# Layer 1's output projection: a fifth unit by seven products, and a new order of the products

## The chip, the core and the metric

The kernel runs on one core of one Trainium2 chip. Its time is device time in microseconds (us), from one execution of the whole program; three timed runs of the kernel before gave a median of 1409.27 us (1408.67 to 1409.78). Beside them stands one profiled execution, whose trace all durations below come from.

The engines are TensorE (PE; PEld is its loading of stationary operands), VectorE (DVE), ScalarE (ACT), GpSimd (POOL) and SyncE (SP). Each works through its own instructions in the order in which the program has them. POOL and SP here mostly issue DMA transfers.

## The reference, cut to what matters

A model of two layers on 512 tokens of width 1024, in float32. Each layer is a mixer (dilated attention in layer 0, an mLSTM in layer 1) and a SwiGLU block; a last RMS norm follows. What the change touches is the second matrix product of the SwiGLU block of layer 1, with the residual and the norm behind it:

```python
def swiglu(xn, w_in, w_out):
    gu = xn @ w_in
    return (jax.nn.silu(gu[..., :D_FF]) * gu[..., D_FF:]) @ w_out
...
        h = h + swiglu(rms_norm(h, ffn_norm[i]), ffn_w_in[i], ffn_w_out[i])
    return rms_norm(h, final_norm)
```

So the output projection is a product of a hidden matrix of 512 x 2816 with `w_out` of 2816 x 1024.

## The kernel before

**Precision.** Every matrix product is computed as three products of halves: each float32 operand is split into a high part (a rounding copy on ACT, L209 for weights, L1120 for activations) and a low part (a subtraction on DVE, L210 for weights, L1109 for activations), and high x high, high x low and low x high are added up in PSUM (`SPLITS`).

**The layer's first product.** `ffn_in` computes the hidden matrix `hid` in 11 pairs of 128-row chunks (`hid[0]` to `hid[10]`), the last eight of them by seven products instead of eight (L1017). While it runs, `during` (L1248) prepares sums of the hidden matrix for the second product, and the last of its steps already prepare that product's first operands.

**The output projection.** `output_products` (L1087) plans it for both layers. Take a quarter problem: rows k of `w_out` in two halves, tokens in two halves of 256, output columns in two halves of 512. Eight products of quarters would be needed; with sums and differences of the operands seven do (P1 to P7), whose results are added up in PSUM. A *unit* u is one such set of seven products; it couples the row pairs `hid[u]` and `hid[UNITS + u]`. With `UNITS = 4` in layer 1, four units cover 8 of the 11 row pairs, and the remaining three (`REST`) are computed plainly, for each of the two column halves: "first" (columns 512 and up) and "second" (columns below 512). Layer 0 has `sums_of_rows` true and `UNITS = 5`.

One product is 12 matmuls of 128 x 128 by 128 x 512 in layer 1 (`multiply_half`, L1697: two token tiles, two k-chunks, three splits); a plain rest item is 24 in the loop. The order is written out by hand (L1265 to L1269): P1 of all units, P5 and P2 in turn, P6 of all units, P7 with the "first" rest items between, P3, P4, and the three "second" rest items at the end.

**Where the sums of weights come from.** Each unit has one weight tile `T` (`f1T` in the trace), loaded by SP at P1 (L1174). P1, P5, P6 and P4 split it in place. Behind the split at P1 and at P5 it is negated on ACT (L1166) and another row block is added to it by a DMA with addition that POOL issues (L1163, 512 KB); at P6 it is only negated; at P7 a freshly loaded block is added to it on DVE (L1189: the block's tile becomes the sum) and POOL adds a further block to `T` for P4. P2, P3, P7 and the rest load their block by SP into one of three buffers `wraw` (L201). The split results, high and low, take one of three buffers each (`whi`, `wlo`), given out in the order of the items: the split of item i + 2 can begin when PE has finished item i - 1.

**What limits the order.** `prepare` (L1271) puts the preparation of an item two items ahead of its product (`AHEAD = 2`); a scheduler then fixes one order of instructions for each engine, by its own estimates.

**PSUM.** P1 and P2 add into `c11`, P5 and P3 into `p5`, P6, P7 and P4 into `u_`. At four points a finished sum is carried over: `copy_banks(u_, c11)` behind the last P1 and `copy_banks(c22, p5)` behind the last P5 (ACT), `add_banks((0, 1), u_)` behind the last P6 and `add_banks((2, 3), u_)` in `after_p7` behind the last P7 (DVE, L1726, `ht <- finu`). They are keyed by the last unit's number, 3. The next product that writes to `u_` must wait for the DVE addition that reads it. `outputs` (behind P4_0 and P4_1) adds the residual for columns 512 and up and squares it for the norm.

**The end.** The last three items (`TAIL = 3`, before: second_0 to second_2) are not run in the loop but tile by tile (from L1750 on): token tiles 0, 1, 2, then tile 3 in two halves of 256 columns, so that a tile's residual (L1709), square (L1711), root (L1771, Newton step L1772 to L1774), scaling (L1776 on ACT, L1778 on DVE, gains L1713 on POOL) and output DMA run beside the next tile's matmuls. A "product" among the last items concerns tiles 2 and 3 only:

```python
            todo = [e for e in last if tb >= 2 or e[0] == "rest"]
```

Of the kernel before, what the change touches and what calls it, by code (L numbers as in the profile page):

```python
# [12 lines left out]
F32R = mybir.dt.float32r  # L13
# [4 lines left out]
P = 128  # L18

SEQ = 512  # L20
# [51 lines left out]
def tile_hybrid_dilated_attn_mlstm(  # L72
# [5 lines left out]
    x = x[0]  # L78
# [6 lines left out]
    xp = pool(ctx, "act")  # L85
# [258 lines left out]
    h = [hp.tile([P, SEQ], F32, tag="h", name="h%d" % k, bufs=KC + 1) for k in range(KC)]  # L344
# [745 lines left out]
    def output_products(layer, fp, wo, sums_of_rows):  # L1090
# [3 lines left out]

        UNITS = 5 if sums_of_rows else 4
        TAIL = 3
        REST = range(2 * UNITS, FC // 2)
        hid, ops, whl, sums, tw, w8 = [], {}, {}, [], [], []  # L1100
# [4 lines left out]
        def half(pi, t):  # L1105
            return hid[pi][:, :, t * HALF:(t + 1) * HALF]

        def subtract(out, x, y):
            nc.vector.tensor_tensor(out, x, y, op=ALU.subtract)  # L1109

        def split_operand(name, u, src):

            i = UNITS * (PARTS.index(name) % 3) + u
            nm = "f%d%s_%d" % (layer, name, u)
            if i < 2 * len(PRODUCTS):
                t = fp.tile([P, 2, 2, HALF], F32R, tag="op%d" % i, name=nm)
                hi, lo = t[:, 0], t[:, 1]
            else:
                hi, lo = [fp.tile([P, 2, HALF], F32R, tag="gu0", name=nm, bufs=3) for _ in range(2)]
            nc.scalar.activation(hi, src, AF.Copy)  # L1120
            subtract(lo, src, hi.bitcast(F32))
            ops[name, u] = [[t[:, k] for k in range(2)] for t in (hi, lo)]
# [31 lines left out]
        def prepare_product(name, u):  # L1154
            nm = "f%d%s_%dw" % (layer, name, u)
            view = lambda t: t.rearrange("p (k n) -> p k n", k=2)

            def load(hk, n):
                return load_chunk(weight_rows(hk * UNITS + u, n), [P, 2, 512], nm)[0]

            def add_rows(to, hk, n):

                nc.gpsimd.dma_start(view(to), weight_rows(hk * UNITS + u, n), accum_op=ALU.add)  # L1163

            def negate(x):
                nc.scalar.activation(x, x, AF.Copy, scale=-1.0)  # L1166
            if name == "P1":
                if u < 4:
                    if u % 2 == 0:
                        w8.append(fp.tile([P, 2, 1024], F32, tag="w8", name="f%dT%d" % (layer, u), bufs=2))  # L1170
                    tw.append(w8[-1][:, u % 2])
                else:
                    tw.append(fp.tile([P, 1024], F32, tag="t1", name="f%dT%d" % (layer, u)))
                nc.sync.dma_start(view(tw[u]), weight_rows(u, 0))  # L1174
            t = tw[u]
            in_place = ("P1", "P6", "P3") if sums_of_rows else ("P1", "P5", "P6", "P4")
            if sums_of_rows and name == "P5":
                prepare_first_sum(u, t, nm)
                return
            raw = t if name in in_place else load(*ROWS[name])  # L1180
            if sums_of_rows:

                if name == "P7":
                    nc.vector.tensor_tensor(raw, raw, t, op=ALU.add)
                    add_rows(t, 1, 0)


            elif name == "P7":
                nc.vector.tensor_tensor(raw, raw, t, op=ALU.add)  # L1189
                add_rows(t, 1, 0)  # L1190
            whl[name, u] = split_chunk((raw, 1024, view, nm))
            if sums_of_rows and name == "P1":

                for i in {0: (0,), 1: (1,), UNITS - 1: range(2, UNITS)}.get(u, ()):
                    load_first_sum(i)
            if sums_of_rows:
                if name == "P6":
                    negate(t)
            elif name in ("P1", "P5"):
                negate(t)  # L1200
                add_rows(t, int(name == "P5"), 1)
            elif name == "P6":
                negate(t)

            if (name, u) in ops:
                return
            if name == "P1":
                split_operand(name, u, half(u, 0))
            elif name == "P2":
                split_operand(name, u, half(UNITS + u, 0))  # L1210
            elif name == "P5":
                split_operand(name, u, sums[u])
            elif name == "P6":
                split_operand(name, u, half(u, 1))

                subtract(sums[u], half(u, 1), half(u, 0) if sums_of_rows else half(UNITS + u, 1))
            elif name == "P7":
                split_operand(name, u, sums[u])
            elif name == "P3":
                if not sums_of_rows:  # L1220
                    subtract(half(u, 1), half(UNITS + u, 0), half(u, 1))
                split_operand(name, u, half(UNITS + u, 1) if sums_of_rows else half(u, 1))
            elif name == "P4":
                if sums_of_rows:
                    subtract(half(UNITS + u, 0), half(UNITS + u, 0), half(u, 1))
                split_operand(name, u, half(UNITS + u, 0 if sums_of_rows else 1))

        def prepare_rest(n, pi):
            if pi not in ops:
                i = pi - REST[0]  # L1230
                two = lambda name, *tags: [fp.tile([P, SEQ], F32R, tag=tg, name="f%dh%s%d" % (layer, name, pi), bufs=bufs)
                                           for tg, bufs in tags]
                if sums_of_rows:
                    hi, lo = two("h", ("gu1", 2), ("gu1", 2)), two("l", ("u2", 1), ("v5", 1))
                else:

                    p, tag = (fp, "op%d" % (3 * UNITS + i)) if i < 2 else (xp, "x%d" % (pi - 4))
                    t = p.tile([P, 2, SEQ], F32R, tag=tag, name="f%dhh%d" % (layer, pi))
                    hi = [t[:, k] for k in range(2)]
                    lo = two("l", *((("u2", 1), ("v5", 1)) if i == 0 else (("gu%d" % (2 - i), 1 + i),) * 2))  # L1240
                for k in range(2):
                    nc.scalar.activation(hi[k], hid[pi][:, k], AF.Copy)
                    subtract(lo[k], hid[pi][:, k], hi[k].bitcast(F32))
                ops[pi] = hi, lo
            whl[n, pi] = split_chunk(load_chunk(weight_rows(pi, n), [P, 2, 512], "f%dw%d_%d" % (layer, n, pi)))

        def during(j, i):
# [12 lines left out]
            if j == FC - 2 and i == 6:  # L1260
# [4 lines left out]
        order = ("P1_0 P1_1 P1_2 P1_3 P1_4 P5_0 P2_0 P5_1 P2_1 P6_0 P5_2 P2_2 P6_1 P5_3 P2_3 P6_2 P5_4 P2_4 P6_3 P6_4 "  # L1265
                 "P7_0 first_0 P7_1 P7_2 P3_0 P7_3 P3_1 P7_4 P3_2 P3_3 P4_0 P3_4 P4_1 P4_2 P4_3 P4_4 second_0"
                 if sums_of_rows else
                 "P1_0 P1_1 P1_2 P1_3 P5_0 P2_0 P5_1 P2_1 P5_2 P2_2 P5_3 P2_3 P6_0 P6_1 P6_2 P6_3 P7_0 first_0 P7_1 first_1 "
                 "P7_2 first_2 P7_3 P3_0 P3_1 P3_2 P3_3 P4_0 P4_1 P4_2 P4_3 second_0 second_1 second_2").split()  # L1269
        items = []  # L1270
        for e in order:  # L1271
            name, i = e.split("_")
# [27 lines left out]
    with ExitStack() as fctx:  # L1300
        fp = pool(fctx, "ffn0")
        hid, during, prepare, work = output_products(0, fp, ffn_w_out[0], True)
# [24 lines left out]
        old, h = h, []  # L1327
# [16 lines left out]
        def first_tiles():  # L1344
            for m in range(4):
                natural(m, F[0][m])
        last = work(product, plain, {("P1", 4): lambda: copy_half(0), ("P5", 4): lambda: copy_half(1),
                                     ("P6", 4): lambda: add_sum(0), ("P7", 4): lambda: add_sum(1),
                                     ("P4", 2): first_tiles})
# [8 lines left out]
    with ExitStack() as mctx:  # L1358
# [138 lines left out]
        i = 0  # L1497
# [154 lines left out]
    with ExitStack() as fctx:  # L1652
        fp = pool(fctx, "ffn1")
        dp = pool(fctx, "scratch1", space=bass.MemoryType.DRAM)
        R = 32
        hid, operands, prepare, work = output_products(1, fp, ffn_w_out[1], False)
# [17 lines left out]
        for n in (1, 0):  # L1674
            for tb in range(TB):
                t = ht[tb, n] = hp.tile([P, SEQ], F32, tag="h", name="ht%d_%d" % (tb, n), bufs=KC + 1)
# [18 lines left out]
        c11, u_ = [bank("s", "c11") for _ in range(2)], [bank("acc", "u") for _ in range(2)]  # L1695
# [24 lines left out]
        def copy_banks(to, src):  # L1720
            for m in range(2):
                nc.scalar.activation(to[m], src[m], AF.Copy)

        def add_banks(tbs, src):
            for m, tb in enumerate(tbs):
                nc.vector.tensor_tensor(ht[tb, 1], src[m], ht[tb, 1], op=ALU.add)  # L1726
# [12 lines left out]
        def plain(n, pi, a, w):  # L1739
            for t in range(2):  # L1740
                multiply_half(((c11, u_), (p5, c22))[n][t], a, t, w)

        last = work(product, plain, {("P1", 3): lambda: copy_banks(u_, c11), ("P5", 3): lambda: copy_banks(c22, p5),
                                     ("P6", 3): lambda: add_banks((0, 1), u_), ("P7", 3): after_p7,
                                     ("P4", 0): lambda: outputs((0, 1), p5), ("P4", 1): lambda: outputs((2, 3), c22)})

        rest_of = bank("o", "last")
        t = ht[TB - 1, 0][:, 256:]
# [55 lines left out]
```

## Time and profile before

| | us |
|---|---|
| median of the three timed runs | 1409.27 (1408.67 to 1409.78) |
| the profiled execution's own time | 1408.68 |
| its span, first to last instruction | 1406.9 |
| PE busy in the span | 1394.5 (99%) |
| DVE / ACT / POOL busy | 1054.9 (75%) / 665.4 (47%) / 149.0 (11%) |
| granted TensorE clock, mean | 0.999 |
| output projection of layer 1 on PE, first to last matmul | 1290.59 to 1399.94 |

How to read it: the profiled execution took 1.8 us more than its span, which lies around the span and isn't seen in it. A busy share is an average over all stages. Matmuls are pipelined, so that one of 128 x 512 shows a duration of 0.39 us while the next starts 0.23 us later; what a product costs is therefore read from starts, not from durations. Rows of a timeline give start, duration, engine, line, operation, output <- inputs, and in brackets how long the engine sat idle before and what released it.

### The profile page before, as it was taken

How to read it: one execution, taken by the hardware profiler on the slowest of the kernel's cores; microseconds unless marked ns; L12 is line 12 of the kernel's file. 1: busy time of each engine (PE TensorE's matmuls, PEld its weight loads, DVE VectorE, ACT ScalarE, POOL GpSimd, SP SyncE). 2: the span in 40 equal slices, each digit the busy share in tenths (PEclk: the TensorE clock that was granted, in tenths of full speed). 3: DMA queues.
4: the chain of work that ended last, by engine and by line, in shares of the span. 5: the costliest groups of instructions: out<-in, count | busy, mean ns of one | idle time of the engine just before them, and what ended most of it. 6: DMA issues, size and time to landing. Idle time of an engine off the chain costs nothing. (4 is left out here: it accounts for less than half of the span.)

```text
span 1406.9 us, 21243 instructions
## 1 busy us (share of the span) xinstructions
PE 1394.5 (99%) x8226; PEld 1237.5 (88%) x8226; DVE 1054.9 (75%) x1832; ACT 665.4 (47%) x1111; POOL 149.0 (11%) x222
## 2 busy tenths in 40 slices
PE   9999999999999999999999999999999999999998
PEld 7888888888888888999999998888888899999886
DVE  7866557566567298777877898998758888887875
ACT  5333224224225253444576463786534444458744
POOL 1011011002002000000000101113101240001111
PEclk9999999999999999999999999999999999999999
DMA  6346245335434455433263733234333553335861
GB/s 195 102 109 203 76 117 160 118 106 131 159 105 121 157 143 156 106 120 119 68 180 85 161 110 103 82 89 106 96 100 105 168 158 117 120 102 125 174 192 60
DMA packets 137277, 176.02 MB, mean 125 GB/s; under 512 B 8596, under 2 KB 111316, under 8 KB 137176
## 3 DMA queue, kind: packets, MB, share of 16 engines
q1 hardware_dynamic: 121392, 134.17, 30.8%
q0 software_dynamic: 14128, 39.37, 12.5%
q8 instruction: 64, 1.05, 0.3%
q10 hardware_dynamic: 1656, 1.12, 0.2%
q14 instruction: 37, 0.30, 0.1%
HBM read 158.91 MB, written 15.73 MB: 124 GB/s over the span
## 5 line engine op out<-in xcount | busy, mean ns | idle before, releaser
L240 PE MATMUL f0j<-n_h,f0j_h 128*128 128x512 f32 x96 | 37.5, 390 | 0.0
L240 PE MATMUL f1j<-n_h,f1j_h 128*128 128x512 f32 x96 | 37.5, 390 | 0.0
L240 PE MATMUL f0j<-n_h,f0j_l 128*128 128x512 f32 x96 | 37.4, 389 | 0.0
L240 PE MATMUL f1j<-n_h,f1j_l 128*128 128x512 f32 x96 | 37.4, 389 | 0.0
L240 PE MATMUL f0j<-n_l,f0j_h 128*128 128x512 f32 x96 | 37.3, 389 | 0.0
L240 PE MATMUL f1j<-n_l,f1j_h 128*128 128x512 f32 x96 | 37.3, 389 | 0.0
L1138 POOL DMA_DIRECT2D f0S<-in_ffn_w_out_dram x10 | 8.7, 866 | 265.1 <-ACT f0P L1120 155.1
L1163 POOL DMA_DIRECT2D f1T<-in_ffn_w_out_dram x12 | 14.6, 1217 | 179.0 <-ACT f1T L1166 151.6
L1665 POOL DMA_DIRECT2D hD<-hB x32 | 20.7, 653 | 96.4 <-DVE hB L1662 96.4
L539 DVE TENSOR_TENSOR rot<-rot,sinr 32x1024 f32<-32x1024 f32 x24 | 28.9, 1206 | 0.0
L240 PE MATMUL mo<-n_h,mo_k_h 128*128 128x512 f32 x64 | 25.3, 396 | 0.0
L240 PE MATMUL mo<-n_h,mo_k_l 128*128 128x512 f32 x64 | 25.3, 395 | 0.0
L240 PE MATMUL mo<-n_l,mo_k_h 128*128 128x512 f32 x64 | 25.1, 393 | 0.0
L240 PE MATMUL mwo<-yo_l,mwo_k_h 128*128 128x512 f32 x64 | 25.1, 393 | 0.0
L240 PE MATMUL mqk<-n_h,mqk_k_h 128*128 128x512 f32 x64 | 25.1, 392 | 0.0
L240 PE MATMUL awo<-ao_h,awo_k_h 128*128 128x512 f32 x64 | 25.1, 392 | 0.0
L240 PE MATMUL mqk<-n_l,mqk_k_h 128*128 128x512 f32 x64 | 25.1, 392 | 0.0
L240 PE MATMUL mwo<-yo_h,mwo_k_l 128*128 128x512 f32 x64 | 25.0, 391 | 0.0
L240 PE MATMUL mqk<-n_h,mqk_k_l 128*128 128x512 f32 x64 | 25.0, 390 | 0.0
L240 PE MATMUL awo<-ao_h,awo_k_l 128*128 128x512 f32 x64 | 25.0, 390 | 0.0
L240 PE MATMUL awo<-ao_l,awo_k_h 128*128 128x512 f32 x64 | 24.9, 390 | 0.0
L240 PE MATMUL mwo<-yo_h,mwo_k_h 128*128 128x512 f32 x64 | 24.8, 391 | 0.0
(2282 smaller groups left out, 5461.3 us busy)
## 6 DMA issues: line engine op xcount, KB each, us to landing
f0j_w<-in_ffn_w_in_dram SPq DMA_DIRECT2D x28, 512.0 KB, 4.4
f1j_w<-in_ffn_w_in_dram SPq DMA_DIRECT2D x28, 512.0 KB, 4.9
f1T<-in_ffn_w_out_dram POOLq DMA_DIRECT2D x12, 512.0 KB, 7.1
awo_k_w<-in_attn_w_out_dram SPq DMA_DIRECT2D x8, 512.0 KB, 6.8
mv_k_w<-in_mlstm_w_in_dram SPq DMA_DIRECT2D x8, 512.0 KB, 3.7
mqk_k_w<-in_mlstm_w_in_dram SPq DMA_DIRECT2D x8, 512.0 KB, 3.7
mo_k_w<-in_mlstm_w_in_dram SPq DMA_DIRECT2D x8, 512.0 KB, 3.8
mwo_k_w<-in_mlstm_w_out_dram SPq DMA_DIRECT2D x8, 512.0 KB, 3.7
```

The lines of the kernel that those rows point to most:

```text
L240: nc.tensor.matmul(acc, whl[a][:, k, m * P:(m + 1) * P], pairs[b][kk], start=(kk == 0 and (a, b) == SPLITS[0]), stop=(kk == nk - 1 and (a, ...
L539: nc.vector.tensor_tensor(sh, sh, sinr.unsqueeze(1).to_broadcast([R, 2, SEQ]), op=ALU.mult)
L1138: nc.gpsimd.dma_start(t, src[1][:, ks], accum_op=ALU.add)
L1163: nc.gpsimd.dma_start(view(to), weight_rows(hk * UNITS + u, n), accum_op=ALU.add)
L1665: nc.gpsimd.dma_start(hD[k // 4].rearrange("(b i) x -> i b x", i=R)[:, :, c0:c0 + R], t[R * a_:R * (a_ + 1)])
```

## The change

In layer 1 `UNITS` becomes 5, so that five units (35 products) cover ten row pairs and one pair is left for the rest. The written order changes: P5 and P2 in turn as before, then P6 and P3 in turn, then the five P7 with the one "first" rest item behind the second of them, then P4 and the one "second" item. The difference `half(u, 1) - half(UNITS + u, 1)` that P7 needs is now formed with P5 instead of with P6, since P3 overwrites `half(u, 1)` earlier now. The keys of the carry-overs follow the last unit (4). The last three items are now P4_3, P4_4 and second_0. The buffers of the rest's operands are those that layer 0 uses.

```diff
-        UNITS = 5 if sums_of_rows else 4
+        UNITS = 5
         TAIL = 3
         REST = range(2 * UNITS, FC // 2)
...
             elif name == "P5":
                 split_operand(name, u, sums[u])
+
+                subtract(sums[u], half(u, 1), half(UNITS + u, 1))
             elif name == "P6":
                 split_operand(name, u, half(u, 1))
-
-                subtract(sums[u], half(u, 1), half(u, 0) if sums_of_rows else half(UNITS + u, 1))
+                if sums_of_rows:
+                    subtract(sums[u], half(u, 1), half(u, 0))
...
         def prepare_rest(n, pi):
             if pi not in ops:
-                i = pi - REST[0]
                 two = lambda name, *tags: [fp.tile([P, SEQ], F32R, tag=tg, name="f%dh%s%d" % (layer, name, pi), bufs=bufs)
                                            for tg, bufs in tags]
-                if sums_of_rows:
-                    hi, lo = two("h", ("gu1", 2), ("gu1", 2)), two("l", ("u2", 1), ("v5", 1))
-                else:
-
-                    p, tag = (fp, "op%d" % (3 * UNITS + i)) if i < 2 else (xp, "x%d" % (pi - 4))
-                    t = p.tile([P, 2, SEQ], F32R, tag=tag, name="f%dhh%d" % (layer, pi))
-                    hi = [t[:, k] for k in range(2)]
-                    lo = two("l", *((("u2", 1), ("v5", 1)) if i == 0 else (("gu%d" % (2 - i), 1 + i),) * 2))
+                hi, lo = two("h", ("gu1", 2), ("gu1", 2)), two("l", ("u2", 1), ("v5", 1))
...
-                 "P1_0 P1_1 P1_2 P1_3 P5_0 P2_0 P5_1 P2_1 P5_2 P2_2 P5_3 P2_3 P6_0 P6_1 P6_2 P6_3 P7_0 first_0 P7_1 first_1 "
-                 "P7_2 first_2 P7_3 P3_0 P3_1 P3_2 P3_3 P4_0 P4_1 P4_2 P4_3 second_0 second_1 second_2").split()
+                 "P1_0 P1_1 P1_2 P1_3 P1_4 P5_0 P2_0 P5_1 P2_1 P5_2 P2_2 P5_3 P2_3 P5_4 P2_4 P6_0 P3_0 P6_1 P3_1 P6_2 P3_2 "
+                 "P6_3 P3_3 P6_4 P3_4 P7_0 P7_1 first_0 P7_2 P7_3 P7_4 P4_0 P4_1 P4_2 P4_3 P4_4 second_0").split()
...
-        last = work(product, plain, {("P1", 3): lambda: copy_banks(u_, c11), ("P5", 3): lambda: copy_banks(c22, p5),
-                                     ("P6", 3): lambda: add_banks((0, 1), u_), ("P7", 3): after_p7,
+        last = work(product, plain, {("P1", 4): lambda: copy_banks(u_, c11), ("P5", 4): lambda: copy_banks(c22, p5),
+                                     ("P6", 4): lambda: add_banks((0, 1), u_), ("P7", 4): after_p7,
                                      ("P4", 0): lambda: outputs((0, 1), p5), ("P4", 1): lambda: outputs((2, 3), c22)})
```

## The prediction

> **What bounds the kernel now.** I read the page first (span, busy shares, clock), then the chain of waits that ended last, then the output projection by itself.
>
> ```profile
> span 1406.9 us, 21243 instructions
> PE 1394.5 (99%) x8226; PEld 1237.5 (88%) x8226; DVE 1054.9 (75%) x1832; ACT 665.4 (47%) x1111; POOL 149.0 (11%) x222
> PEclk9999999999999999999999999999999999999999
> ```
>
> PE is busy throughout, at a full clock in all 40 slices: time is won only where PE gets fewer matmuls, and lost where it must wait. The chain that ended last, from 1361 us on (start, length, engine, output, line, count), shows the price of a product and the end:
>
> ```profile
> 1361.63 10.88 PE finp L1703 x48
> 1372.51 10.88 PE finu L1703 x48
> 1383.39 8.16 PE finc L1759 x36
> 1391.55 4.09 PE finu L1759 x18
> ...
> 1402.20 0.72 ACT ht L1776
> ```
>
> 48 matmuls are four products: 10.88 / 4 = 2.72 us for one, 0.2267 us for one matmul; nothing but PE stands in the chain. The windows of this stage give the other engines (columns: length, then busy us and instruction count of PE, PEld, DVE, ACT, POOL, then clock, DMA share, GB/s):
>
> ```profile
> 1290.60:1300.00 9.40, 9.40 (x44) 7.78 (x43) 5.41 (x6) 9.40 (x14) 3.64 (x3) 1.00 0.93 142
> 1300.00:1320.00 20.00, 20.00 (x90) 16.57 (x89) 19.15 (x25) 15.74 (x21) 4.86 (x4) 1.00 0.99 202
> 1345.00:1383.20 38.20, 38.20 (x170) 31.64 (x169) 27.44 (x38) 17.59 (x24) 3.31 (x3) 1.00 0.46 129
> ```
>
> ACT is full in the first window (9.40 of 9.40), DVE nearly full in the second (19.15 of 20.00), yet PE loses nothing: both run ahead.
>
> **The change, part by part.**
>
> *Matmuls.* Before: 28 products x 12 + 3 rest pairs x 2 x 24 = 480. After: 35 x 12 + 2 x 24 = 468. Twelve go: 12 x 0.2267 = **-2.72 us**, the whole of what can be won here.
>
> *Work of DVE and ACT.* Back-to-back rows give what an instruction holds DVE:
>
> ```profile
> 1305.40 0.68 DVE L1109 TENSOR_TENSOR f1P<-f1hid,f1P 128x512 fp32r<-128x512 f32 x1
> 1306.00 1.22 DVE L210 TENSOR_TENSOR f1P_1w_l<-f1P_1w_w,f1P_1w_h 128x1024 fp32r<-128x1024 f32 x1
> 1307.14 0.68 DVE L1109 TENSOR_TENSOR f1P<-f1hid,f1P 128x512 fp32r<-128x512 f32 x1
> 1340.27 1.22 DVE L1189 TENSOR_TENSOR f1P_2w_w<-f1P_2w_w,f1T 128x1024 f32<-128x1024 f32 x1
> ```
>
> 0.60 us for 512 elements, 1.14 for 1024. A unit has seven weight splits, seven operand splits, two differences and one L1189: 8 x 1.14 + 9 x 0.60 = 14.5 us beside 7 x 2.72 = 19.0 on PE. A rest pair has two splits each: 3.5. In all 4 x 14.5 + 3 x 3.5 = 68.5 before and 76.0 after, beside some 106 of PE: hidden in the sum, so what counts is where it bunches. P1 has 1.74 a product, P5/P2 and P6/P3 in turn 2.04 each (differences included), P4 1.74, P7 **2.88**: only the P7 run exceeds 2.72. ACT's densest stretch, P1, is a rounding, a negation and a copy a product, and the first window shows that ACT keeps up there; the early copies for the rest give way to those of the fifth unit. The moved difference costs 0.60 beside P5 (counted); `during` takes two subtractions more, where seven products hold PE: both at nothing; uncovered, 0.6 each. T of the fifth unit uses a tile free before the neighbouring loads, so SP, in order, isn't held. SP's loads stay at 22 (16 + 6 before, 20 + 2 after); POOL's additions go from 12 to 15, and except in the P7 run each has at least eight products until it is needed.
>
> *The wait that is added.* P4_0 now follows P7_4 directly and writes `u_`, which `add_banks((2, 3))` on DVE must first read; before, four P3 (10.88 us) lay between. The trace shows the same handover at the last P6:
>
> ```profile
> 1329.99 1.23 DVE L210 TENSOR_TENSOR f1P_0w_l<-f1P_0w_w,f1P_0w_h 128x1024 fp32r<-128x1024 f32 x1 [0.85 <-ACT f1P_0w_h L209]
> 1331.25 0.37 SPq L201 DMA_DIRECT2D f1w_w<-in_ffn_w_out_dram  x1
> 1331.62 1.06 ACT L209 ACTIVATE f1w_h<-f1w_w 128x1024 fp32r<-128x1024 f32 x1 [0.19 <-PE finu L1703]
> 1332.71 1.23 DVE L210 TENSOR_TENSOR f1w_l<-f1w_w,f1w_h 128x1024 fp32r<-128x1024 f32 x1 [1.49 <-ACT f1w_h L209]
> 1333.86 1.28 DVE L1726 TENSOR_TENSOR ht<-finu,ht 128x512 f32<-128x512 f32 x2
> 1334.37 0.39 PE L1703 MATMUL finp<-f1w_l,f1hh 128*128 128x512 f32 x1
> 1334.59 0.50 PE L1703 MATMUL finu<-f1P_0w_h,f1P 128*128 128x512 f32 x1
> ```
>
> P6_3 was issued by 1334.14, P7_0 began at 1334.59: 0.45 us late, because a weight split (freed by PE at 1331.4) stood on DVE ahead of the two additions. Two matmuls of the rest filled the gap. The changed kernel, built, has the same order on DVE (the split for P4_1, then the two additions) and nothing on PE between P7_4 and P4_0: at least 0.45 us. More if DVE comes late, which I follow from the end of P6_4, called 0: P3_4 ends at 2.72, P7_0 5.44, P7_1 8.16, the rest item 13.6, P7_2 16.3, P7_3 19.0, P7_4 21.8. The load times needed:
>
> ```profile
> f1T<-in_ffn_w_out_dram POOLq DMA_DIRECT2D x12, 512.0 KB, 7.1
> f1w_w<-in_ffn_w_out_dram SPq DMA_DIRECT2D x6, 512.0 KB, 4.6
> DMA to landing us min/median/max: 3.7/4.6/7.8
> ```
>
> (The last line is of the `f1w_w` loads; a load leaves SP 0.1 us behind the split that frees its buffer, rows 1329.99 and 1331.25.) On DVE in its order: additions of P6_4 until 1.0; L1189 of P7_1 until 2.1; two operands until 3.3; P7_1's split (ACT's rounding ends 3.3) until 4.5, which frees the buffer for P7_3's block; one operand, the rest's split, L1189 and operand of P7_2 until 8.0. P7_3's block, issued at 4.6, lands at 9.3: DVE **waits 1.3 us**. L1189 until 10.5, split of P7_2 11.7, operand and split of P7_3 13.4, L1189 and operand of P7_4, operands of P4_0 and P4_1 16.4, split of P7_4 17.6 (needed at 19.0), two output additions 18.8, split of P4_0 19.9, small ones and an operand 20.9, split of P4_1 22.0, first addition 22.7. P4_0 could have begun at 21.76: **+1.0 us**. Bounds: 0.45 if DVE has caught up; with the longest load, 7.8 instead of 4.6, 1.0 + 3.2 = 4.2. I take 1.0, by the median load. Behind the additions on DVE wait the splits of P4_2 (done 25.1, needed 28.2), so nothing else is late.
>
> *The end.* Before, each tile had 18 matmuls (4.08 us) and its chain of root and scaling went beside the next tile's:
>
> ```profile
> 1383.43 1.06 ACT L209 ACTIVATE f1w_h<-f1w_w 128x1024 fp32r<-128x1024 f32 x1 [1.66 <-PE finu L1703]
> 1384.52 1.23 DVE L210 TENSOR_TENSOR f1w_l<-f1w_w,f1w_h 128x1024 fp32r<-128x1024 f32 x1 [0.67 <-ACT f1w_h L209]
> 1387.51 0.69 DVE L1709 TENSOR_TENSOR ht<-finc,ht 128x512 f32<-128x512 f32 x1 [1.76 <-PE finc L1759]
> 1388.97 1.28 ACT L1771 ACT_TABLE_LOAD   x1
> 1391.29 0.75 DVE L1778 SCALAR_TENSOR_TENSOR ht<-ht,fr,gbc 128x512 f32<-128x512 f32 x1
> 1392.02 0.39 ACTq L1777 DMA_DIRECT2D out_dram<-ht  x1
> 1399.66 0.28 PE L1759 MATMUL finlast<-f1w_h,f1hl 128*128 128x256 f32 x1
> 1400.02 0.41 DVE L1709 TENSOR_TENSOR ht<-finlast,ht 128x256 f32<-128x256 f32 x1
> 1401.20 0.20 ACT L1771 ACTIVATE fr<-fv 128x1 f32<-128x1 f32 x1 [0.23 <-DVE fv L1769]
> ```
>
> The last weights' low part was ready 2.52 us behind the last loop product (1383.23 to 1385.75). After, the built order puts 11 matmuls of P4_3, P4_4 and high parts ahead of the first one that needs it: 11 x 0.2267 = 2.49 us, so **+0.15** at most for the semaphore. But tiles 0 and 1 now have six matmuls each and end close together; their chains (1387.51 to 1392.04 here, 4.5 us with the table load) meet on ACT and DVE with tile 2 and the halves of tile 3. Laid out from the rows, in the built order: additions of tiles 0 and 1 until 5.8 us behind the last loop product, second square 6.6, table load 7.9, roots and Newton steps 9.4, scaling on DVE until 10.8, output DMAs on ACT until 11.5, root of tile 2 11.7, its scaling 13.4, only then the root of tile 3 (14.1) and its scaling at 14.9, 3.4 us behind the last matmul (11.4). Before it was 2.3 (1399.94 to 1402.20). So **+1.2**; bounds: 0, if the two DMA issues hold ACT for nothing and tile 3 isn't late, and 2.2, if tiles 0 and 1 go one after the other.
>
> *Sum*: -2.72 + 1.0 + 0.15 + 1.2 = -0.4 us on the profiled execution's 1408.68 (span 1406.9 and 1.8 around it), so 1408.3. The median of the runs lies 0.6 higher, 1409.27: **1408.9 us**.
>
> **The rivals.** (A) *The gain arrives nearly whole*: DVE has caught up by P7_4 (0.45) and the chains of the end interleave (0): -2.72 + 0.45 = -2.3, 1407.0. For it: DVE's idle time before (27.44 busy of 38.20); against it the order, which holds the additions behind a split.
> (B) *DVE becomes the bound in the P7 run* and the time ends on the other side: P7_3's block must wait for the buffer that P7_1's split frees; at 7.8 us landing the whole DVE queue behind it shifts by 3.2 and the wait at P4_0 is 4.2: 1408.9 + 3.2 = 1412.1. It turns slower than before once the block lands 0.4 us later than 4.6. For it: POOL's additions travel at the same time; against it: the median, and that up to 2 us later P7_2's split, then due at 13.6, still comes in time (11.7 + 1.9).
> (C) *POOL's additions come late.* POOL issues one in 1.2 us, in the window with DVE at 19.15 of 20.00 as elsewhere:
>
> ```profile
> 1301.33 1.21 POOL L1163 DMA_DIRECT2D f1T<-in_ffn_w_out_dram  x1 [2.68 <-ACT f1T L1166]
> 1349.79 1.21 POOL L1163 DMA_DIRECT2D f1T<-in_ffn_w_out_dram  x1 [6.56 <-DVE f1P L1109]
> ```
>
> If one took five times as long, 6.0 us, the five behind P7's L1189 would end at 26 and the last land 5.9 later, 32; P4_4's split wants it at 28.4: some 3.5 us late, 1412.4. With 1.2 us it lands at about 22, 6 us early, and costs nothing. The Trainium skill, "SBUF — State Buffer" (the "DVE blocks DMA" trap, ahead of "A bandwidth-pool intuition"), says that GpSimd can't write the descriptors of its DMAs while VectorE runs in a mode that takes both ports, with 620 ns grown to 3100 in its example; by that rule (C) would be the forecast. The two rows speak against it here.
>
> **How the numbers follow.** Forecast 0.63, (A) 0.17, (B) 0.14, (C) 0.02, something unseen 0.04, half of it slower. The range leaves out the bounds' far ends: 1406.9 (A) to 1411.3, three quarters of the way to (B). About 0.2%, 2.8 us, is what a measurement of this kernel can tell from no change. Twelve matmuls are 2.72, so faster by over 0.2% needs a gain elsewhere: 0.04. Slower by over 0.2% (beyond 1412.1) is the upper half of (B) with (C): 0.12. Within 0.2%: 0.84.
>
> **What would show it.** 468 matmuls in the projection and no gap on PE until the last P7; then DVE idle ahead of an L1189 for a DMA, and about 1 us without a matmul ahead of P4_0, with L1726 as releaser; last matmul some 1.5 us earlier than before, and 3 to 4 us from it to the last scaling on ACT. The forecast is wrong if PE waits on a weight split (DVE or a load bounds), or if the last scaling still follows the last matmul by 2.3 us (A).

## The result and the profile after

The changed kernel takes **1411.9 us** (median; 1411.1 to 1413.2) against 1408.85 for the kernel before in runs on the same chip (1408.5 to 1410.0): 3.05 us more, a ratio of 1.0019 [1.0013, 1.0026]. It is slower. The forecast of 1408.9 was 3.0 us too low, and the time lies just beyond the range. The profiled execution took 1411.98 us, with a span of 1410.2.

The page of the kernel after, its first lines, its row of the granted clock and the shares of the chain that ended last:

```profile
span 1410.2 us, 21261 instructions
PE 1393.6 (99%) x8214; PEld 1236.4 (88%) x8214; DVE 1065.2 (76%) x1843; ACT 671.6 (48%) x1120; POOL 153.2 (11%) x225
PEclk9999999999999999999999999999999999999998
PE 31%; DVE 5%; ACT 1%; issue 1%; DMA 0%; ACTq 0%; DVEq 0%
```

PE has 8226 - 8214 = 12 matmuls fewer, as foreseen. Three small signs say where to look: the last digit of the clock has gone from 9 to 8 (that slice also holds the clock's fall behind the last matmul), DVE's share of the chain has risen from 4% to 5%, and a DMA now stands in it. Which DMA it is, the chain of waits of the kernel after says (start, length, engine, output, line, count):

```profile
1350.39 2.73 PE finp L1697 x12
1353.14 1.07 ACT f1P_0w_h L209
...
1359.00 1.16 DVE f1P_1w_l L210
1360.18 6.40 DMA f1P_3w_w<-in_ffn_w_out_dram
1366.67 1.22 DVE f1P_3w_w L1189
...
1378.02 1.22 DVE f1P_1w_l L210
1379.24 0.61 DVE ht L1720
1379.98 10.03 PE finu L1697 x36
```

Read it upward: the matmuls of P4_0 (1379.98) were released by the addition that reads `u_` (L1720; L1726 before); that addition stood behind a long row of DVE work, and DVE had last been idle for the block of P7_3, whose load took 6.40 us and began only when the split of P7_1 had freed its buffer. The timeline of DVE in the kernel after shows the same (in brackets the idle time ahead and its releaser):

```profile
1358.92 1.23 DVE L210 TENSOR_TENSOR f1P_1w_l<-f1P_1w_w,f1P_1w_h 128x1024 fp32r<-128x1024 f32 x1
...
1362.94 0.69 DVE L1109 TENSOR_TENSOR f1P<-f1S,f1P 128x512 fp32r<-128x512 f32 x1
1366.67 1.22 DVE L1189 TENSOR_TENSOR f1P_3w_w<-f1P_3w_w,f1T 128x1024 f32<-128x1024 f32 x1 [3.04 <-DMA f1P_3w_w<-in_ffn_w_out_dram]
...
1378.02 1.22 DVE L210 TENSOR_TENSOR f1P_1w_l<-f1T,f1P_1w_h 128x1024 fp32r<-128x1024 f32 x1
1379.15 1.28 DVE L1720 TENSOR_TENSOR ht<-finu,ht 128x512 f32<-128x512 f32 x2
```

From the end of the 3.04 us of idling DVE has no idle time until the additions. On PE, the timeline of the kernel after around the end of P7_4:

```profile
1377.30 0.39 PE L1697 MATMUL finu<-f1P_4w_h,f1P 128*128 128x512 f32 x1
1379.98 0.57 PE L1697 MATMUL finu<-f1P_0w_h,f1P 128*128 128x512 f32 x1 [2.30 <-DVE ht L1720]
...
1384.40 0.39 PE L1697 MATMUL finu<-f1P_1w_h,f1P 128*128 128x512 f32 x1
```

The next matmul would have started at 1377.30 + 0.23 = 1377.53, so the gap costs 2.45 us. And the twelve matmuls of P4_0 then take 1384.40 - 1379.98 = 4.42 us instead of 2.72. The windows of the kernel after say why; columns as before, the clock third from the right:

```profile
1376.00:1377.00 1.00, 1.00 (x6) 0.84 (x5) 1.00 (x2) 1.00 (x5) 0.00 (x0) 1.00 1.17 193
1378.00:1379.00 1.00, 0.00 (x0) 0.00 (x0) 1.00 (x2) 0.83 (x1) 0.00 (x0) 1.00 0.58 197
1380.10:1380.30 0.20, 0.20 (x1) 0.15 (x2) 0.20 (x1) 0.00 (x0) 0.00 (x0) 0.76 0.05 20
1381.00:1382.00 1.00, 1.00 (x3) 0.77 (x3) 1.00 (x2) 0.00 (x0) 1.00 (x1) 0.50 0.00 0
1382.00:1383.00 1.00, 1.00 (x4) 0.74 (x3) 1.00 (x3) 0.00 (x0) 1.00 (x1) 0.50 0.00 0
1383.60:1383.80 0.20, 0.20 (x2) 0.17 (x2) 0.20 (x1) 0.00 (x0) 0.00 (x0) 0.95 0.00 0
```

PE's busy column is full in both windows at 0.50, with three or four matmuls started where there were six: a full busy column says nothing about speed, the clock column does. A mean of 0.76 in 0.20 us means that 0.48 of it was at half clock, so the clock fell at 1380.20; 0.95 puts its return at 1383.62. That is 3.42 us at half clock, worth 1.71 us of PE.

The end, on ACT and DVE of the kernel after:

```profile
1398.97 2.43 DVE L1772 SCALAR_TENSOR_TENSOR ht<-ht,fr,gbc 128x512 f32<-128x512 f32 x2
1401.10 0.28 PE L1753 MATMUL finlast<-f1w_h,f1hl 128*128 128x256 f32 x1
1403.22 1.18 DVE L1772 SCALAR_TENSOR_TENSOR ht<-ht,fr,gbc 128x512 f32<-128x512 f32 x1
1405.50 0.72 ACT L1770 ACTIVATE ht<-ht,fr 128x512 f32<-128x512 f32 x1 [0.80 <-DVE fr L1768]
```

From the last matmul's end (1401.38) to the last scaling are 4.12 us; before, 2.26.

**The account.** The projection begins at 1290.59 before and at 1290.36 after; executions differ by up to a microsecond there, so I count from the projection's first matmul. To the start of the last matmul it was 109.07 us and is 110.74; to the last scaling 111.61 and 115.14, **+3.53**:

| | foreseen | measured |
|---|---|---|
| twelve matmuls fewer | -2.72 | -2.72 |
| gap ahead of P4_0 | +1.0 | +2.45 |
| P4_0 at half clock | nothing | +1.70 |
| small gaps elsewhere on PE | +0.15 | +0.24 (the remainder) |
| last matmul to last scaling | +1.2 | +1.86 |
| sum | -0.4 | +3.53 |

The spans differ by 3.3 and the medians by 3.05, so the account of the one profiled execution is about right in size.

### The profile page after: what moved, and what is told of

Its sections match the earlier page's. It is cut to its first block, busy times and chain, and to the rows that moved or that the text cites. A ratio compares the mean times of both kernels' runs of the same rounds, so it can differ in the third digit from the quotient of the medians.

```text
span 1410.2 us, 21261 instructions
## 1 busy us (share of the span) xinstructions
PE 1393.6 (99%) x8214; PEld 1236.4 (88%) x8214; DVE 1065.2 (76%) x1843; ACT 671.6 (48%) x1120; POOL 153.2 (11%) x225
## 5 line engine op out<-in xcount | busy, mean ns | idle before, releaser
L1163 POOL DMA_DIRECT2D f1T<-in_ffn_w_out_dram x15 | 18.2, 1212 | 198.3 <-ACT f1T L1166 157.4
```

## The experiments

The theory behind all of them: the gap ahead of P4_0 comes from the load of P7_3's block, which waits for a buffer; the clock falls because of the gap; the end is dearer because chains meet there. The rivals: DVE simply has too much work in the P7 run; the clock, or the new order as a whole, does harm by itself.

**1. Own buffers for the late P7 blocks.** P7_2 to P7_4 load into operand tiles that are free by then, and not into the three shared buffers; the work and its order stay.

```diff
+            if layer == 1 and name == "P7" and u >= 2:
+                raw = fp.tile([P, 1024], F32, tag="op%d" % (8 + u), name=nm + "_w")
+                nc.sync.dma_start(view(raw), weight_rows(u, 0))
+            else:
+                raw = t if name in in_place else load(*ROWS[name])
```

> The blocks for P7_2, P7_3 and P7_4 go to operand tiles that are free by then, instead of to the three shared load buffers; all else is the changed kernel. Theory (P7_3's block is issued late because P7_1's split must free its buffer, DVE waits 3.0 us for it, the additions ahead of P4_0 come 2.45 us late, and PE's clock drops behind that gap): no DMA wait on DVE in the P7 run, a gap ahead of P4_0 of 0.4 to 1.0 us, matmuls of P4_0 at 0.227 us, 1408.2 to 1408.8 us. Rival (DVE simply has too much work in the P7 run, 2.88 us a product): the gap stays above 2 us, 1411.5 to 1412.

Measured: 1409.36 us against 1409.37 for the kernel before, ratio 0.9999 [0.999, 1.0007]. The whole loss of 3 us is gone, but nothing is won. In this run's timeline DVE doesn't idle for a DMA in the P7 run (the row of P7_3's block has no wait ahead of it), and PE has a gap at P4_0 of 0.59 us between starts beyond the usual 0.23, at full clock:

```profile
1364.59 1.22 DVE L1193 TENSOR_TENSOR f1P_3w_w<-f1P_3w_w,f1T 128x1024 f32<-128x1024 f32 x1
...
1379.06 0.47 PE L1701 MATMUL finu<-f1P_0w_h,f1P 128*128 128x512 f32 x1 [0.43 <-DVE ht L1724]
```

What is left of the gap is the split that stands ahead of the two additions on DVE, the lower bound of 0.45 in the prediction. DVE's work is the same as in the changed kernel, so too much of it is not the cause. The time came out above the expected 1408.2 to 1408.8. The kernel before was 0.5 us slower in these runs than in those that the expectation started from, and the end still takes 4.11 us: -2.72 + 0.59 + 0.24 + 1.86 is about zero. To the last scaling it is 111.57 us, 3.57 less than in the changed kernel: 1.86 of the gap and 1.7 of the clock.

**2 to 4. The gap filled, its cause left alone.** Between P7_4 and P4_0 stand matmuls by a stationary matrix of zeros, into a PSUM sum that they leave as it is. They don't make P4_0 start sooner; they only shorten the time in which PE does nothing. First eleven, then five, then two:

```diff
+            for _ in range(11):
+                nc.tensor.matmul(c11[0], zeros_r, operand_of_rest()[0][0], start=False, stop=False,
+                                 skip_group_check=True)
             add_banks((2, 3), u_)
```

> Eleven matmuls with a stationary operand of zeros, added to c11 (they change nothing), stand between P7_4 and P4_0: PE has 2.5 us of work where it had a gap of 2.45 us. Theory (the slow P4_0 is the clock falling because of the gap): P4_0 begins when it did, 2.4 to 2.6 us behind P7_4, but runs at 0.227 us a matmul with the granted clock at 1.00: 1.7 us less, about 1410.2 us. Rival (P4_0 is slow for another reason, its PSUM banks being read by DVE or its operands coming late): P4_0 takes 4.4 us as before, 1411.9 us.

> As the run with eleven, but only five matmuls of zeros: a gap of some 1.3 us is left, as long as the 1.26 us gap ahead of m2num in this kernel. Theory (a gap of 1.3 us is not enough for the clock to fall): full pace, about 1410.2 us. Rival (any gap above some 1 us lets it fall): P4_0 slow again, 1411.5 to 1412 us.

> Two matmuls of zeros between P7_4 and P4_0: a gap of about 2.0 us, between the 1.0 us that left the clock alone and the 2.45 us that didn't. If what counts is a gap of some 2 us, the clock falls again: 2.9 to 3.3 us above the kernel before. If it takes nearly the whole 2.45 us, P4_0 runs at 0.227 us a matmul: 1.5 to 2 us above.

| filling matmuls | PE idle ahead of P4_0 | clock in P4_0 | median, before | ratio | projection's start to last scaling |
|---|---|---|---|---|---|
| none (the changed kernel) | 2.45 | 0.50 | 1411.9, 1408.85 | 1.0019 [1.0013, 1.0026] | 115.14 |
| 2 | 1.77 | 1.00 | 1410.89, 1409.04 | 1.0014 [1.0006, 1.0023] | 113.21 |
| 5 | 1.0 | 1.00 | 1411.11, 1409.37 | 1.0010 [1.0001, 1.0019] | 113.12 |
| 11 | none | 1.00 | 1411.18, 1409.37 | 1.0011 [1.0002, 1.0020] | 113.47 |

With two of them, P4_0 starts as late as ever, and the window behind it has six matmuls at full clock:

```profile
1378.06 0.63 PE L1685 MATMUL finc<-f1hh,zeros_r 128*128 128x512 f32 x2
1380.28 0.47 PE L1703 MATMUL finu<-f1P_0w_h,f1P 128*128 128x512 f32 x1 [1.60 <-DVE ht L1726]
```

```profile
1381.00:1382.00 1.00, 1.00 (x6) 0.79 (x6) 1.00 (x2) 0.00 (x0) 1.00 (x1) 1.00 0.00 0
```

From the projection's start P4_0 begins at 89.62 us in the changed kernel and at 89.30, 89.23 and 89.66 with two, five and eleven: the wait is the same to within 0.4 us, and the clock differs. So the fall of the clock is a cost of its own that hangs on how long PE idles. To the last scaling the traces differ by 1.7 to 2.0 us; less the earlier starts of P4_0 that is 1.6 to 1.7. The medians say the same in sign and less in size (some 1.2 us, with intervals that overlap). Of the expected times, 1410.2 with eleven and with five was missed by 0.9 to 1.0 us, of which 0.5 is the kernel before, slower on this chip; with two, 1.85 us above the kernel before was within the expected 1.5 to 2.

A rival is chance: the place of the gap among the moments at which the clock can change. In the changed kernel's trace it changes at 1380.20, at 1383.62 and, behind the last matmul, at 1404.10; these are 3.42 and 20.48 us apart, and 20.48 is six times 3.413. In the run with two, the fall behind the end is at 1405.15, and seven times 3.413 us earlier is 1381.26. If the clock is decided in such stretches, end to end, both gaps lay whole within one. The windows of these two stretches, first the changed kernel's with its fall behind the end, then the run with two:

```profile
1376.79:1380.20 3.41, 1.11 (x5) 0.64 (x5) 3.41 (x9) 2.04 (x3) 0.00 (x0) 1.00 0.60 147
1404.05:1404.15 0.10, 0.00 (x0) 0.00 (x0) 0.10 (x1) 0.00 (x0) 0.00 (x0) 0.74 0.00 0
```

```profile
1377.84:1381.26 3.42, 1.82 (x8) 1.22 (x7) 3.42 (x6) 1.34 (x2) 0.42 (x1) 1.00 0.39 111
1405.00:1405.30 0.30, 0.00 (x0) 0.00 (x0) 0.00 (x0) 0.00 (x0) 0.00 (x0) 0.75 0.01 0
```

PE was busy for 1.11 us of the one and for 1.82 of the other, so it was not a luckier place that kept the clock up with two. Other places weren't tried, but the seventeen timed runs of the changed kernel hint at them. Eleven have a mean clock of 0.997 and took 1411.73 to 1413.15 us; the six with 0.998 are the fastest, 1411.06 to 1411.47. Of the 98 timed runs of the other variants one has 0.997. As 3.42 us at half clock lower the mean over 1410 us by 0.0012, it seems that the clock fell in some executions of the changed kernel and not in others, which would also make the medians differ by less than the traces. Only one of them was profiled, so this isn't shown, and neither is the limit between 1.77 and 2.45 us.

**5. The order of the kernel before, with five units.** All P6, then P7 with the rest item behind the first, then P3, P4:

```diff
-                 "... P6_0 P3_0 P6_1 P3_1 P6_2 P3_2 P6_3 P3_3 P6_4 P3_4 P7_0 P7_1 first_0 P7_2 P7_3 P7_4 P4_0 ..."
+                 "... P6_0 P6_1 P6_2 P6_3 P6_4 P7_0 first_0 P7_1 P7_2 P7_3 P7_4 P3_0 P3_1 P3_2 P3_3 P3_4 P4_0 ..."
```

> Five units, but in the order of the kernel before (all P6, then P7 with the rest item behind the first, all P3, all P4, the second rest item last): the change without its new order. Theory (the gap belongs to P4_0 standing directly behind P7_4; the end's crowd belongs to the fifth unit, that is to the tail with one rest item): five P3 lie ahead of P4_0, no gap above 0.3 us, clock 1.00, the last scaling 4 us behind the last matmul as in the changed kernel: -2.7 + 1.9 = 0.5 to 1.0 us below the kernel before. Rival (five P7 nearly on end overload DVE by themselves, wherever they stand): PE waits for weight splits within the P7 run, 1 to 3 us above.

Measured: 1411.94 us against 1409.04, ratio 1.0020 [1.0011, 1.0029]. The expectation missed. Five P3 do take the place of the gap at P4_0, but now the P7 run itself stalls. The waits of PE in this run (what waited, for whom, us in total, times, longest) and the timeline of its DVE:

```profile
PE finu L1697 <- DVE f1P_3w_l L210: 0.9, 1, 0.9
PE finp L1697 <- DVE f1P_1w_l L210: 0.8, 1, 0.8
```

```profile
1358.47 1.23 DVE L1189 TENSOR_TENSOR f1P_4w_w<-f1P_4w_w,f1T 128x1024 f32<-128x1024 f32 x1 [4.13 <-DMA f1P_4w_w<-in_ffn_w_out_dram]
```

DVE idles 4.13 us for P7_4's block, and PE then waits for weight splits. From this alone it could also be DVE's load of 2.88 us a product in a longer run of P7. The next run decides that.

**6. The old order, with own buffers.** Experiment 5 with the edit of experiment 1.

> Five units in the order of the kernel before, with the blocks of P7_2 to P7_4 in operand tiles that are free by then. Theory (there too it is the shared load buffers that make DVE late: it waited 4.1 us for P7_4's block): that wait goes and with it most of PE's stalls of 1.2 us at P7_3 and 1.3 us at P3_1; what is left is the crowd at the end: 0.3 to 0.9 us below the kernel before. Rival (DVE has too much work in the P7 run): the stalls stay, 2 to 3 us above the kernel before.

Measured: 1408.69 us against 1409.05, ratio 0.9998 [0.9989, 1.0007]. The stalls are gone but for two gaps of some 0.1 us, with the same work on DVE, and DVE has P7_4's block without a wait:

```profile
1354.05 1.22 DVE L1193 TENSOR_TENSOR f1P_4w_w<-f1P_4w_w,f1T 128x1024 f32<-128x1024 f32 x1
```

So the buffers bound the P7 run in this order too. The last matmul starts 106.58 us behind the first, 2.49 sooner than before: nearly all of the 2.72. The end takes it back (4.11 instead of 2.26 us), and the median's 0.36 us can't be told from no change.

**7. The plain item as a cover.** The changed kernel, with second_0 between P7_4 and P4_0 instead of last:

```diff
-                 "... P7_0 P7_1 first_0 P7_2 P7_3 P7_4 P4_0 P4_1 P4_2 P4_3 P4_4 second_0").split()
+                 "... P7_0 P7_1 first_0 P7_2 P7_3 P7_4 second_0 P4_0 P4_1 P4_2 P4_3 P4_4").split()
```

> The second rest item moves from the end to between P7_4 and P4_0; the last three items are P4_2, P4_3 and P4_4, so that tiles 0 and 1 are complete long before the end. Theory (the added wait and the crowd at the end are all that ate the twelve matmuls): the first half of the rest item, 2.72 us into c11, covers the additions, no gap, full clock, and the last scaling follows the last matmul by 2.3 us: 1408.85 - 2.7 = 1406.1, up to 1406.6 us. Rival (the end is bound by DVE and ACT work that only moves): the last scaling still 3.5 to 4 us behind the last matmul, 1407.5 to 1408 us.

Measured: 1407.74 us against 1409.37, ratio 0.9988 [0.9979, 0.9997]: faster than before by 1.6 us, less than expected. The item's 24 matmuls hide the late addition, so gap and clock are gone; and as the last three items are now products, which concern tiles 2 and 3 only, tiles 0 and 1 are finished early and the last scaling follows the last matmul by 2.25 us, as before. What is missing stands in this run's timelines:

```profile
1367.32 1.23 DVE L1189 TENSOR_TENSOR f1P_3w_w<-f1P_3w_w,f1T 128x1024 f32<-128x1024 f32 x1 [2.78 <-DMA f1P_3w_w<-in_ffn_w_out_dram]
...
1391.58 0.50 PE L1753 MATMUL finu<-f1P_3w_l,f1P 128*128 128x512 f32 x1 [0.61 <-DVE f1P_3w_l L210]
```

DVE has still lost 2.78 us to the load, and PE pays 0.77 of that later, ahead of the low part of P4_3.

**8. Both.** Experiment 7 with the buffers of experiment 1.

> The early second rest item together with own tiles for the blocks of P7_2 to P7_4. Theory (with 2.72 us of rest item in front, DVE's 2.8 us wait for the block is covered already): the DMA wait on DVE goes, the time stays that of the early rest item alone, 1.4 to 2.0 us below the kernel before. Rival (DVE's lateness is carried on into the last splits, where PE waits 0.77 us for P4_3's): that gap goes as well, another 0.5 to 0.8 us less.

Measured: **1406.87 us** against 1409.04, ratio 0.9983 [0.9974, 0.9992]. It beats both kernels. The gap ahead of P4_3's low part has gone too, as the rival had it, so it was a late effect of the same load. No wait of PE is left in the projection; first to last matmul take 106.48 us (109.07 - 2.59), and the end is as before:

```profile
1398.01 0.28 PE L1757 MATMUL finlast<-f1P_4w_h,f1P 128*128 128x256 f32 x1
1400.54 0.72 ACT L1774 ACTIVATE ht<-ht,fr 128x512 f32<-128x512 f32 x1 [0.79 <-DVE fr L1772]
```

**9. The end without POOL's part.** Experiment 1, with POOL's multiplication of columns 0 to 511 by the final norm's gains left out (so this kernel leaves out part of the computation):

```diff
-            if n == 0:
-                nc.gpsimd.tensor_tensor(t, t, gbc[0][:, cs], op=ALU.mult)
```

> As the run with own tiles, but POOL's multiplication by the gains of columns 0 to 511 (L1707 in the changed kernel) is left out, so the first half of the output lacks that factor. Theory (the two scalings of tiles 0 and 1 on DVE take 2.43 instead of 1.4 us because POOL reads SBUF beside them): the pair takes 1.3 to 1.5 us, the one of tile 2 0.75 instead of 1.18, the last scaling comes 1.0 to 1.5 us earlier: 1.0 to 1.5 us below the run with own tiles, that is below the kernel before by as much. Rival (they are slow for another reason, or the chain of roots on ACT sets the end): within 0.4 us of the run with own tiles.

Measured: 1408.33 us against 1409.04, ratio 0.9994 [0.9985, 1.0003]; the end takes 3.18 us instead of the 4.11 of experiment 1. That is 0.93 in the traces and 0.7 in the medians, less than the 1.0 to 1.5 expected, and the median can't be told from no change. The scalings of tiles 0, 1 and 2 on DVE, in experiment 1, with POOL's rows:

```profile
1396.36 1.30 POOL L1711 TENSOR_TENSOR ht<-ht,gbc 128x512 f32<-128x512 f32 x1 [0.75 <-ACT fsq L1709]
1396.44 1.77 DVE L1776 SCALAR_TENSOR_TENSOR ht<-ht,fr,gbc 128x512 f32<-128x512 f32 x1
1398.13 0.74 DVE L1776 SCALAR_TENSOR_TENSOR ht<-ht,fr,gbc 128x512 f32<-128x512 f32 x1
1399.89 1.43 POOL L1711 TENSOR_TENSOR ht<-ht,gbc 128x256 f32<-128x256 f32 x2 [2.23 <-ACT fsq L1709]
1400.69 1.18 DVE L1776 SCALAR_TENSOR_TENSOR ht<-ht,fr,gbc 128x512 f32<-128x512 f32 x1
```

and those of tiles 0 and 1 in this run, together:

```profile
1396.14 1.42 DVE L1774 SCALAR_TENSOR_TENSOR ht<-ht,fr,gbc 128x512 f32<-128x512 f32 x2
```

The scaling that overlaps POOL's first row takes 1.77 us and ends 0.55 us behind it (1398.21 and 1397.66); the next, with POOL done, takes 0.74. That of tile 2 takes 1.18 and again ends 0.55 us behind POOL's row (1401.87 and 1401.32). So of the 1.86 us that the end has grown, 0.93 came from DVE being held up while POOL multiplied; the other 0.93 is the remainder, put down to the chains that meet. Experiments 7 and 8, where tiles 0 and 1 end early and POOL multiplies as before, show that all of the 1.86 hangs on that meeting. The Trainium skill, "SBUF — State Buffer" (Who interferes with whom), says that a VectorE instruction with two SBUF inputs contends with a GpSimd instruction that reads SBUF. The trace agrees: with `ht` and `gbc` as inputs the pair takes 2.43 us (1396.44 to 1398.87) where POOL multiplies and 1.42 where it doesn't.

## Why the prediction was wrong, step by step

- **Matmuls, -2.72: right.** In experiment 8, where nothing else is in the way, 2.59 of it arrives on PE.
- **Work of DVE and ACT, nothing: right as a sum.** Experiments 1 and 6 have the same work on DVE; what PE waits there, 0.59 us in experiment 1, is one split that stands ahead of the additions, not the amount of work. The loads' buffers bunched the P7 run, not the work.
- **The wait that is added: the mechanism was right, its size was the step that failed.** The prediction followed DVE from the end of P6_4 and came to the right place: P7_3's block behind P7_1's split, DVE idle, the additions late. It took the median load, 4.6 us, out of rows from 3.7 to 7.8; the load took 6.4. P6_4 is the product behind the chain's 1350.39 and ends at 1353.12 + 2.72 = 1355.84; the first addition was done at 1379.24 + 0.61 = 1379.85, 24.0 us later instead of 22.7, and P7_4 was over at 1377.53, 21.7 as laid out. That is 2.3, and 2.45 with the 0.13 until the matmul starts, instead of 1.0. That is rival (B), at about half its price. That the measured 1411.9 lies near (B)'s 1412.1 is luck: (B) had one wait of 4.2 us, and the run had a gap of 2.45 and 1.70 by the clock. In that stretch POOL issues its additions as well:

```profile
1358.74 1.20 POOL L1163 DMA_DIRECT2D f1T<-in_ffn_w_out_dram  x1 [8.74 <-DVE f1P_1w_w L1189]
1363.56 1.20 POOL L1163 DMA_DIRECT2D f1T<-in_ffn_w_out_dram  x1 [3.62 <-DVE f1P_2w_w L1189]
```

  The block travelled from 1360.18 to 1366.6, beside both. In experiment 1 the blocks of P7_2 to P7_4, loaded earlier and P7_3's with no addition under way, took 3.9 to 4.0 us. Over all eleven traces, loads of 512 KB in the projection took 3.7 to 5.2 us with no such addition in flight (13 loads whose landing the trace has), 4.1 to 8.2 beside two (28) and 4.3 to 9.8 beside three or four (43). That the additions slow a load fits this, but no run took them away alone, so it isn't shown as the cause. The median that the prediction took came from six loads, the two shortest of which (3.70 and 3.73 us, issued at 1364.27 and 1367.21) had no addition beside them; the load in question had two.
- **A term that the sum did not have: the clock, +1.70.** The prediction read full clock in all 40 slices of the kernel before and took it for granted. Experiments 2 to 4 show that it hangs on the gap. Had the gap been 1.0 us as forecast, there would have been no such term (1.0 us left the clock at 1.00); the error in the load's time brought both. The Trainium skill, "TensorE: Matmul & The Clock Gate" (What's actually happening), says that the clock halves behind an idle window of about 3.4 us, that the window runs freely, and that the clock comes back behind a busy one. The 3.42 us at half clock agree with that window. Its rule of no idle gaps over about 3.4 us (HAM oscillation) does not: 2.45 us were enough here.
- **The end, +1.2 and +0.15: right in kind, too small.** The chains of tiles 0 and 1 do meet with those of tiles 2 and 3; 0.93 is left for that. The other 0.93, DVE held up by POOL's multiplication, was missing: the layout used the scaling's 0.75 us from a stretch in which POOL was idle. 1.86 lies within the bounds of 0 to 2.2.
- **(A) fell:** DVE had not caught up by P7_4, and the chains of the end didn't interleave. **(C) fell:** POOL issued its additions in 1.20 us as before, none late. The rule quoted for it is about a mode of VectorE that takes both ports; no row here shows DVE in such a mode, so (C) didn't follow from the rule.
- **What would show it:** no gap on PE until the last P7, then DVE idle ahead of an L1189 for a DMA, and L1726 as releaser at P4_0 all came as written. "About 1 us" was 2.45, the last matmul was 1.67 later within the projection instead of 1.5 earlier, and from its end to the last scaling it was 4.12, just above the 3 to 4.

In short, the step that failed is the wait ahead of P4_0: sized by a load of 4.6 us that took 6.4, it was put at 1.0 and was 2.45, and the clock behind it was put at nothing and cost 1.70. The gap alone had a bound of 4.2 us that holds 2.45; the clock had none. Without its 1.70 the time would, by this account, have been about 1410.2, within the range.

## What to carry to other kernels

Where PE bounds and a change takes matmuls away, the gain can be lost at the handovers that the removed or moved work covered: look for who must read a PSUM sum before the next product writes it, and keep an independent item at that place. Before an order is blamed, look at the buffers: a load whose buffer is freed by a late instruction, and on which an engine that works in order must wait, delays everything behind it, and a few idle tiles may cure that. A gap on PE can cost more than itself, as the one of 2.45 us did here, and matmuls that compute nothing, put into it, can be cheaper than idling.

## What was not expected of the hardware

- A PE gap of 2.45 us was followed by 3.42 us at half clock, which cost 1.7 us more; gaps of 1.0 and 1.77 us at the same place left the clock at 1.00.
- A scaling of 128 x 512 on DVE with two SBUF inputs took 0.74 us alone; beside a multiplication on POOL it took 1.18 and 1.77, and both times ended 0.55 us behind POOL's.
- A load of 512 KB took 6.4 us in a stretch with POOL's additions, against 3.7 to 5.2 for loads with no such addition in flight; that the additions held it up isn't shown.
